# A fifth tile for loaded weight pieces, tables kept per mixer, and a later split of the attention probabilities

## The chip, the cores and the metric

The kernel runs on one core of a Trainium2 chip. The metric is the device time of one execution in microseconds (us); the time of a kernel is the median of its runs. Engines go by the profile's names: PE is the matrix engine (TensorE), PEld its loading of stationary operands, DVE is VectorE, ACT is ScalarE, POOL is GpSimd, and SP is SyncE, which here only issues transfers. "pm" is a PSUM tile of a projection.

## The reference

Two layers of a decoder trunk, 256 tokens of width 2048, all in float32:

```python
for l in range(DEPTH):
    h = rms_norm(x, mix_norm[l])
    if l % 2 == 0: h = mixer_ab(h, ...)   # causal gMLP (8 heads) beside HGRN2 (8 heads), then w_out
    else:          h = mixer_c(h, ...)    # forgetting attention, 16 heads of 128, output gate, then w_out
    x = x + h
    x = x + conv_ffn(rms_norm(x, ffn_norm[l]), ...)   # hidden 5632, causal width-3 convolution, silu(a) * b
```

The attention of one head, in blocks of 128 queries, is `p = softmax(q k^T * scale + c_t - c_s)` under a causal mask, and `o = p v`; q and k are normalised over a head's 128 values, c is the running sum of the log of a forget gate. The output is the residual stream after both layers.

## The kernel before

**Weights in three products.** All large products are made with float32 split in two: a weight piece w, 128 x 1024 and 512 KB, is loaded by a transfer of the SP queue (`weights`, L200), ACT copies it rounded into wh (L187), DVE makes the rest wl = w - wh (L188), and PE makes three products, wh with the high half of the activations, wl with the high half, wh with the low half (L362, L363, L364 in `project_four`; L343 to L345 in `project_tok`; L318 in `project`; L238 and L262 in the first projection). A piece takes 12 matmuls of 512 columns. `three` gives a piece its tiles: w from a pool with 4 slots, wh and wl from one with 3 each; inside the attention mixer each fourth piece has wh and wl in a further slot, and in the MLPs two of five pieces have all three tiles in a further pool with 2 slots each. The transfer of a piece waits until its slot is free, that is until the wl of the piece that had the slot before has been made.

**Order.** The program is written as one sequence of projections. Before each piece `tick` advances one step: it lets each of a few Python generators (for a head, a group of heads, a gate) write its next part of the small work between two pieces. When the program is built, a planner sets the order of the instructions on each engine and each queue from estimated times; edges that are added by hand hold some of it: pieces stay in order, and an operation marked `held` comes on its engine after the wh or wl of the piece last written. On the chip each queue then runs strictly in that order, waiting on semaphores.

**Turning blocks.** Activations come out of the projections with tokens on the partitions and are needed the other way. `blocks` transposes 32 x 32 blocks on DVE (L375), `moves` sends 16 transfers of 32 KB that put them in place (L382), half on SP's queue and half on POOL's. On SP they share the queue with the weights.

**The attention mixer** (`mixer_c`). Four groups of four heads; a group has three projections (q, k, v) of 8 pieces, so 24 steps. `turn_rows` scales, normalises and turns q and k. `attend` takes a pair of heads: high and low halves of q and k (L1050 to L1054), scores (L1061, L1064), forget terms and mask (L1069 to L1073), maximum, exponential with the sums of the rows into rs, 32 x 32 transposes into ptmp (L1087), 16 moves on POOL's queue into pt (L1096); then it lets `LAG + 2`, that is 8, steps pass, and splits the turned probabilities: ph on ACT (L1105), pl on DVE (L1106). One step later follow the products with v (L1114, L1117) and two copies on ACT (L1121). A second pair starts 5 steps after the first. After the groups come four projections for the output gate (w_cg), each followed by a `gate` that turns its rows and multiplies the heads' output (L1200) into yc, which is split (L414, L416); the output projection (w_co) reads yc. Gates after the first begin to multiply when all heads are done.

**Small tiles and tables.** `cst` holds the identity, a triangular mask and the causal mask of the attention for the whole kernel. In the first mixer `ss`, `Rr` and `sos` are three small tiles (factors of the gMLP's norm, reversed per-token factors, factors of HGRN2's output norm), `junk` holds squares, `tot` (2 slots) the running products of HGRN2's decay, and `ar` (3 slots) mirrored activations. In the attention mixer each of the four groups has a tile `rs` for the sums of its rows.

Of the kernel before, what the change touches and what calls it, by code (L numbers as in the profile page):

```python
# [8 lines left out]
F32 = mybir.dt.float32  # L9
# [3 lines left out]
ALU = mybir.AluOpType  # L13
AX = mybir.AxisListType

P = 128
S = 256
D = 2048
KT = D // P
NH = 8  # L20
CH = 16
# [4 lines left out]
LAG = 6  # L26
# [8 lines left out]
LANE = 64  # L35
SMALL = 4
LEVELS = (64, 32, 16, 8, 4, 2, 1)
NL = len(LEVELS)
# [8 lines left out]
K_ID, K_TRI, K_CM, K_REV = 0, 128, 256, 384  # L47
# [8 lines left out]
def tile_trunk(ctx: ExitStack, tc: tile.TileContext, x, pp_d, cst_d, mlev_d, msk_d,  # L56
               w_v, w_f, w_g, w_i, w_q, w_u, w_abo, w_cf, w_cqkv, w_cg, w_co, w_up, w_dn, spw_d, spb_d, out):
    nc = tc.nc
    V, SC, PE = nc.vector, nc.scalar, nc.tensor
# [9 lines left out]
    def nm(base):  # L69
        count[0] += 1  # L70
        return f"{base}_{count[0]}"
# [6 lines left out]
        xT += [t[:, i] for i in range(n)]  # L78
    part = {c0 + i: (t, i, c0 + n - 1) for t, c0, n in xload for i in range(n)}
    pp = cp.tile([P, -(-NPP // LANE) * LANE], F32, tag="pp", name="pp")  # L80
    cst = cp.tile([P, K_REV], F32, tag="cst", name="cst")
    ones = cp.tile([P, P], F32, tag="ones", name="ones")
    one1 = ones[:, 0:1]

    SC.dma_start(pp[:, 0:C_FFN], pp_d[:, 0:C_FFN])
    V.memset(ones, 1.0)
    ident = cst[:, K_ID:K_ID + P]

    order = mybir.DependencyInfo(mybir.DependencyClass.NoSync, mybir.DependencyReason.DATA)
    epoch = {"set": None, "load": None, "ops": []}  # L90
# [72 lines left out]

    def three(n):
        deep["turn"] += 1
        wpool, pool, nw, ns = wp, wp, 4, 3
        if deep["pool"] is not None:
            if deep["more"] == 2 and deep["turn"] > 12 and deep["turn"] % 5 in (1, 3):
                wpool, pool, nw, ns = deep["pool"], deep["pool"], 2, 2
            elif deep["more"] == 1 and deep["turn"] % 4 == 3:  # L170
                pool, ns = deep["pool"], 1
        w = wpool.tile([P, n], F32, tag="w", name=nm("w"), bufs=nw)
        wh = pool.tile([P, n], F32R, tag="wh", name=nm("wh"), bufs=ns)
        wl = pool.tile([P, n], F32R, tag="wl", name=nm("wl"), bufs=ns)
        return w, wh, wl
# [230 lines left out]
    def held(r, last="wh"):  # L406

        tc.add_manual_dep(r.ins, deep[last].ins.name, order, reason="not before")
# [98 lines left out]
    def mixer_ab(norm):  # L507
# [35 lines left out]
        def fetch_late(*args):  # L543
            r = SC.dma_start(*args)
            tc.add_manual_dep(r.ins, deep["hold"].ins.name, order, reason="queue order")

        fetch_late(cst, cst_d[:, 0:K_REV])
        fetch_late(pp[:, C_FFN:C_CW], pp_d[:, C_FFN:C_CW])
        def wide(n):
            return hp.tile([P, 1024], F32, tag="QK", name=nm(n), bufs=2)  # L550
# [9 lines left out]

        def tables():
            yield
            near, tri = kst[:, (NL - 1) * P:NL * P], cst[:, K_TRI:K_TRI + P]
            held(V.tensor_copy(msk, kst), "wl")
            nc.gpsimd.tensor_tensor(two[:, 0], near, tri, ALU.mult)
            nc.gpsimd.tensor_tensor(two[:, 1], near, two[:, 0], ALU.subtract)
            nc.gpsimd.tensor_tensor(two, two, ident.unsqueeze(1).to_broadcast([P, 2, P]), ALU.add)
            yield
            held(V.tensor_tensor(wt[0], wt[0], cst[:, K_TRI:K_TRI + P].unsqueeze(1)
                                 .to_broadcast([P, NH, P]), ALU.mult), "wl")  # L570

        mg = [keep("mg") for _ in range(NH)]

# [13 lines left out]
                                   wt[1][:, h].unsqueeze(1).to_broadcast([P, 2, P]),  # L587
                                   ALU.mult, ALU.add)

        ss = hp.tile([P, LANE], F32, tag="ss", name="ss")  # L590

        def mixes():
            while norm.Rt is None:
                yield
            for g in (1, 0):
                for T in range(2):
                    yield
                    held(act(cols2(gv[g][:, T]), of_two(last[T]) if g else cols2(gv[0][:, T]), AF.Gelu,
                             scale=norm.Rt[:, T:T + 1]))
            yield  # L600
            for g in (1, 0):
                for T in range(2):
                    i = (2 * g + T) * 4
                    j = hp.tile([P, 512], F32, tag="junk", name=nm("junk"), bufs=1)
                    held(V.tensor_tensor(j, gv[g][:, T], gv[g][:, T], ALU.mult), "wl")
                    V.tensor_reduce(ss[:, i:i + 4], j.rearrange("p (h d) -> p h d", d=P), AX.X, ALU.add)
                    yield
            yield
            rsq(ss[:, 0:2 * NH], ss[:, 0:2 * NH], P)
            for g in range(2):  # L610
                yield
                for T in range(2):
                    i = (2 * g + T) * 4
                    v4 = gv[g][:, T].rearrange("p (h d) -> p h d", d=P)
                    held(V.tensor_tensor(v4, v4, ss[:, i:i + 4].unsqueeze(2).to_broadcast([P, 4, P]),
                                         ALU.mult), "wl")
            yield
            yield
            for h in range(0, NH, 2):
                ps = bank()  # L620
                both = [mix(h + i, ps[:, i * S:(i + 1) * S]) for i in range(2)]
                for m in both:
                    next(m)
                for m in both:
                    next(m, None)
                yield


        Rr = hp.tile([P, LANE], F32, tag="Rr", name="Rr")[:, 0:2]
        rab = hp.tile([P, LANE], F32, tag="rab", name="rab")  # L630
        ra, rb = rab[:, 0:BLK], rab[:, BLK:2 * BLK]

# [67 lines left out]
        depth[0] = 5  # L700

        itoks, left, os_ = [], [NH], []
        sos = hp.tile([P, LANE], F32, tag="so", name="sos")[:, 0:2 * NH].rearrange("p (j t h) -> p j t h", j=2, t=2)


        H = P // 2
# [234 lines left out]
    def mixer_c(norm):  # L941
# [3 lines left out]
        deep.update(pool=es.enter_context(tc.tile_pool(name="cw", bufs=1)), turn=0, more=1)  # L945
        A = norm.a
        w2 = hp.tile([P, KT, CH], F32, tag="w2", name="w2")

        def fetch():
            for _ in range(FORGET):  # L950
# [86 lines left out]
        def attend(hs, q, k, v, o, rs, mark):  # L1037
# [28 lines left out]
            for i, (h, sp) in enumerate(zip(hs, sps)):  # L1066
                c0 = 3 * P * i
                parts = ((c0, c0 + P), (c0 + P, c0 + 3 * P))
                V.scalar_tensor_tensor(scf[:, c0:c0 + P], sp[:, 0:P], ct[:, 0, h:h + 1], cb[:, h % 8, 0:P],  # L1069
                                       ALU.add, ALU.subtract)  # L1070
                V.scalar_tensor_tensor(sc[:, 3 * i + 1:3 * i + 3], view(sp, P, (1, 2), (2, P)), ct[:, 1, h:h + 1],
                                       cb[:, h % 8].rearrange("p (t n) -> p t n", t=2), ALU.add, ALU.subtract)
                V.tensor_tensor(sc[:, 3 * i:3 * i + 3:2], sc[:, 3 * i:3 * i + 3:2],  # L1073
                                cst[:, K_CM:K_CM + P].unsqueeze(1).to_broadcast([P, 2, P]), ALU.add)
                mxs = hp.tile([P, LANE], F32, tag="mxs", name=nm("mxs"), bufs=2)[:, 0:2]
                sms = rs[:, :, h % 4:h % 4 + 1]
                for T, (a, b) in enumerate(parts):
                    V.tensor_reduce(mxs[:, T:T + 1], scf[:, a:b], AX.X, ALU.max, negate=True)
                for T, (a, b) in enumerate(parts):
                    act(scf[:, a:b], scf[:, a:b], AF.Exp, bias=mxs[:, T:T + 1], accum_out=sms[:, T])  # L1080
                sums.append(sms)
# [12 lines left out]
            for a in range(4):  # L1094
# [3 lines left out]
                                        .rearrange("p (m r) -> p m r", m=6))  # L1098
                if a == 1:
                    yield  # L1100
            for _ in range(LAG + 2):
                yield
            pair = [hp.tile([P, 2, S], F32R, tag=n, name=nm(n), bufs=1) for n in ("ph", "pl")]
            near = pt.rearrange("p (i m) q -> p i (m q)", i=2)[:, :, 0:S]
# [28 lines left out]
        def turn_rows(ps, ss, j, dst, mark):  # L1133
# [12 lines left out]
            transposed(lambda T: z[:, T], tmp, dst)  # L1146
            mark.append(steps[0])

        for g in range(CH // 4):
            qkv, mark = [], []  # L1150
            ss = hp.tile([P, 2, 2, LANE // 4], F32, tag="ss", name=nm("ss"), bufs=2)[..., 0:4]
            for j in range(3):
                if g == 0 and j == 2:
                    cd = []
                    queue.append(sums(*forget()))
                if g and j == 2:
                    spread(g)
                ps = early[j] if g == 0 and j < 2 else project_tok(w_cqkv[j * (CH // 4) + g], norm)
                if j == 2:
                    vs = [hp.tile([P, 512], F32R, tag=n, name=nm(n), bufs=2) for n in ("vh", "vl")]  # L1160
                    v1 = hp.tile([P, 512], F32, tag="v", name=nm("v"), bufs=2)
                    SC.activation(cols2(vs[0]), of_two(ps[0]), AF.Copy, scale=Rt[:, 0:1])
                    SC.activation(cols2(v1), of_two(ps[1]), AF.Copy, scale=Rt[:, 1:2])
                    V.scalar_tensor_tensor(cols2(vs[1]), of_two(ps[0]), Rt[:, 0:1], cols2(vs[0]).bitcast(F32),
                                           ALU.mult, ALU.subtract)
                    qkv.append((vs, v1))
                    break
                t = piece("turn", 4)
                start(turn_rows(ps, ss, j, heads(t), mark))
                qkv.append(heads(t))  # L1170
            if g == 0:
                columns(cd[1])
            os_.append(heads(piece("o", CH // 4)))
            rss.append(hp.tile([P, LANE], F32, tag="rs", name=nm("rs"), bufs=CH // 4)[:, 0:8]
                       .rearrange("p (t h) -> p t h", t=2))
            queue.extend(attend((h, h + 1), *qkv, os_[g], rss[g], mark) for h in range(4 * g, 4 * g + 4, 2))

        room, places = [], [("big", 4, 1)] + 2 * [("vh", 1, 2), ("vl", 1, 2)] + 4 * [("o", 2, CH // 4)]
# [300 lines left out]
```

## Time and profile before

| | us |
|---|---|
| median of 3 runs | 2173.42 (2173.0 to 2174.6) |
| the profiled execution's own time | 2171.18 |
| its span, first to last instruction | 2169.4 |
| PE busy in the span | 2162.7 |
| PEld, DVE, ACT, POOL busy | 1899.9, 1596.8, 1306.2, 470.1 |

The granted PE clock is full throughout. The span falls into the first mixer (to about 380), the first MLP (to about 1057), the attention mixer (to about 1510) and the second MLP. Busy PE is a modelled time: matmuls overlap, and a matmul's end is computed. So whether PE loses time is read better from the starts of two matmuls than from the idle between them. In the views, "<-" after idle time names what ended it; "SPq" is the queue of SyncE, and "x8" a run of eight merged instructions.

### The profile page before, as it was taken

The page shows a single profiled execution, that of the slowest core. Times are in us where ns is not written, and L with a number is a line of the kernel's source. Part 1 is how long each engine was busy: PE and PEld are TensorE (multiplying, and loading weights), DVE is VectorE, ACT ScalarE, POOL GpSimd, SP SyncE. Part 2 cuts the span into 40 slices and gives each one's busy share as a digit, 9 for nine tenths or more (in the row PEclk, how much of TensorE's full clock was granted, in tenths as well). Part 3 has the DMA queues.
Part 4 walks back from the last instruction along what each step waited for, and adds up shares of the span by engine and source line. Part 5 has one row for each costly group of instructions (what it writes and reads, how often), then busy time and mean ns, then how long its engine had stood idle before and what let it go on. Part 6 is the DMA issues. An engine that isn't in the chain of part 4 may idle for free.

```text
span 2169.4 us, 32511 instructions
## 1 busy us (share of the span) xinstructions
PE 2162.7 (100%) x10874; PEld 1899.9 (88%) x10874; DVE 1596.8 (74%) x2265; ACT 1306.2 (60%) x1903; POOL 470.1 (22%) x865
## 2 busy tenths in 40 slices
PE   9999999999999999999999999999999999999999
PEld 8998888888888888888888888888888888888888
DVE  7788768777577657876987787877776577667766
ACT  6677766666466545654565566666666466456642
POOL 1252231212012002111133444212211012011202
PEclk9999999999999999999999999999999999999999
DMA  8755777877667767776777767777777677766866
GB/s 299 216 174 176 213 227 236 247 231 237 212 214 228 220 215 209 236 234 200 238 229 222 225 213 223 211 242 239 236 233 229 199 236 216 229 213 209 246 214 191
DMA packets 492617, 483.55 MB, mean 223 GB/s; under 512 B 115136, under 2 KB 460368, under 8 KB 492320
## 3 DMA queue, kind: packets, MB, share of 16 engines
q1 hardware_dynamic: 465888, 453.27, 66.4%
q0 software_dynamic: 24832, 25.92, 5.2%
q10 hardware_dynamic: 1728, 2.28, 0.3%
q8 instruction: 85, 1.39, 0.3%
q14 instruction: 84, 0.69, 0.1%
HBM read 435.18 MB, written 2.11 MB: 202 GB/s over the span
## 4 chain that ended last, share of the span: by engine, by line
PE 93%; DVE 2%; DMA 2%; SPq 1%; ACT 1%; issue 1%; POOL 0%; ACTq 0%; DVEq 0%; POOLq 0%
PE pm L363 26%; PE pm L362 26%; PE pm L364 26%; PE pm L343 4%; PE pm L344 4%; PE pm L345 4%; PE pm L318 2%; PE pm L238 1%; SPq L382 1%; DVE wl L188 1%; DMA pt<-ptmp 1%; PE pm L262 0%; DMA w<-in_w_cg 0%; ACT wh L187 0%; DMA w<-in_w_co 0%
## 5 line engine op out<-in xcount | busy, mean ns | idle before, releaser
L188 DVE TENSOR_TENSOR wl<-w,wh 128x1024 fp32r<-128x1024 f32 (+1 forms) x820 | 990.4, 1217 | 451.6 <-ACT wh L187 437.9
L187 ACT ACTIVATE wh<-w 128x1024 fp32r<-128x1024 f32 (+1 forms) x820 | 855.8, 1049 | 615.4 <-PE pm L364 423.0
L363 PE MATMUL pm<-wl,a 128*128 128x512 f32 x1728 | 655.4, 379 | 0.8 <-DVE wl L188 0.8
L362 PE MATMUL pm<-wh,a 128*128 128x512 f32 x1728 | 655.8, 379 | 0.0
L364 PE MATMUL pm<-wh,a 128*128 128x512 f32 x1728 | 654.9, 379 | 0.0
L382 POOL DMA_DIRECT2D zt<-tmp x413 | 223.5, 549 | 1134.1 <-DVE tmp L375 1022.3
L363 PEld LDWEIGHTS pm<-wl,a 128*128 128x128 f32 x1728 | 326.6, 189 | 48.4 <-DVE wl L188 2.5
L362 PEld LDWEIGHTS pm<-wh,a 128*128 128x128 f32 x1728 | 326.6, 189 | 46.3
L364 PEld LDWEIGHTS pm<-wh,a 128*128 128x128 f32 x1728 | 326.6, 189 | 46.2
L362 PE MATMUL pm<-wh,hid 128*128 128x512 f32 x688 | 260.8, 379 | 0.0
L363 PE MATMUL pm<-wl,hid 128*128 128x512 f32 x688 | 260.8, 379 | 0.0
L364 PE MATMUL pm<-wh,hid 128*128 128x512 f32 x688 | 260.8, 379 | 0.0
L343 PE MATMUL pm<-wh,a 128*128 128x512 f32 x416 | 158.7, 381 | 0.0
L344 PE MATMUL pm<-wl,a 128*128 128x512 f32 x416 | 157.8, 379 | 0.1
L345 PE MATMUL pm<-wh,a 128*128 128x512 f32 x416 | 157.8, 379 | 0.0
L363 PEld LDWEIGHTS pm<-wl,hid 128*128 128x128 f32 x688 | 130.0, 189 | 18.5
L362 PEld LDWEIGHTS pm<-wh,hid 128*128 128x128 f32 x688 | 130.0, 189 | 18.4
L364 PEld LDWEIGHTS pm<-wh,hid 128*128 128x128 f32 x688 | 130.0, 189 | 18.4
L382 POOL DMA_DIRECT2D turn<-tmp x160 | 86.9, 550 | 243.3 <-DVE tmp L375 172.7
L1285 ACT ACTIVATE conv<-zt,pp 128x256 f32<-128x256 f32 x176 | 95.8, 589 | 66.3 <-DMA zt<-tmp 43.5
L1286 DVE SCALAR_TENSOR_TENSOR conv<-zt,pp,conv 128x255 f32<-128x255 f32 x176 | 80.2, 480 | 50.0 <-ACT conv L1285 40.4
L375 DVE STREAM_TRANSPOSE tmp<-z 128x512 f32<-128x512 f32 x120 | 97.8, 854 | 5.5 <-ACT z L1271 5.3
(253 smaller groups left out, 2205.7 us busy)
## 6 DMA issues: line engine op xcount, KB each, us to landing
w<-in_w_up SPq DMA_DIRECT2D x352, 512.0 KB, 4.9
w<-in_w_dn SPq DMA_DIRECT2D x176, 512.0 KB, 4.9
w<-in_w_cqkv SPq DMA_DIRECT2D x96, 512.0 KB, 4.8
w<-in_w_abo SPq DMA_DIRECT2D x32, 512.0 KB, 4.8
w<-in_w_cg SPq DMA_DIRECT2D x32, 512.0 KB, 4.7
w<-in_w_co SPq DMA_DIRECT2D x32, 512.0 KB, 4.9
zt<-tmp SPq DMA_DIRECT2D x414, 32.0 KB, 2.6
zt<-tmp POOLq DMA_DIRECT2D x413, 32.0 KB, 2.5
```

The costliest lines, as they stand in the source:

```text
L187: r = deep["wh"] = SC.activation(wh, w, AF.Copy)
L188: deep["wl"] = V.tensor_tensor(wl, w, wh.bitcast(F32), ALU.subtract)
L343: PE.matmul(to_two(ps[T]), ah, h, start=k + i == 0, stop=False)
L344: PE.matmul(to_two(ps[T]), ah, l, start=False, stop=False)
L345: deep["last"] = PE.matmul(to_two(ps[T]), al, h, start=False, stop=k + i == KT - 1)
L362: PE.matmul(to_rows(ps[T]), ah, h, start=not begun and k + i == ks[0], stop=False)
L363: PE.matmul(to_rows(ps[T]), ah, l, start=False, stop=False)
L364: deep["mm"] = deep["last"] = PE.matmul(to_rows(ps[T]), al, h, start=False, stop=not more and k + i == ks[-1] + 1)
L375: V.transpose(tmp.rearrange("p (b m i t) -> p b m i t", b=4, m=4, t=2)[:, :, :, :, T], src(T).rearrange("p (m b j) -> p b m j", m=4, b=4))
L382: queues[(a + b) % len(queues)].dma_start(dst[BLK * b:BLK * (b + 1), :, a * n:(a + 1) * n], tmp[BLK * a:BLK * (a + 1), b * 4 * n:(b + 1) * ...
L1285: held(SC.activation(c, z, AF.Identity, bias=pp[:, cb:cb + 1], scale=w(2)))
L1286: V.scalar_tensor_tensor(c[:, 1:], z[:, :S - 1], w(1), c[:, 1:], ALU.mult, ALU.add)
```

## The change

The pool of loaded pieces w has 5 slots in place of 4, for all pieces that do not use a further pool. Room for it (4 KB on each partition) comes from the small tiles: the constants are no longer kept for the whole kernel (1.5 KB), but loaded by each mixer that reads them, in the first mixer into a slot of `tot` by one transfer on ACT's queue, in the attention mixer into a tile of its own by two transfers of 64 KB on POOL's queue; the squares go into a slot of `ar` in place of `junk` (2 KB); `ss`, `Rr` and `sos` become parts of one tile, and the four `rs` parts of another. And `attend` lets `LAG + 5` steps pass, 11 in place of 8, ahead of the split of the probabilities.

```diff
 def three(n):
-        wpool, pool, nw, ns = wp, wp, 4, 3
+        wpool, pool, nw, ns = wp, wp, 5, 3
 ...
 # tile_trunk
-    cst = cp.tile([P, K_REV], F32, tag="cst", name="cst")
-    ident = cst[:, K_ID:K_ID + P]
 # mixer_ab
-        fetch_late(cst, cst_d[:, 0:K_REV])
+        cst = hp.tile([P, S], F32, tag="tot", name="cst", bufs=2)
+        ident, tri = cst[:, K_ID:K_ID + P], cst[:, K_TRI:K_TRI + P]
+        fetch_late(cst, cst_d[:, 0:S])
-        ss = hp.tile([P, LANE], F32, tag="ss", name="ss")
+        small = hp.tile([P, LANE], F32, tag="ss", name="small")
+        ss = small[:, 0:2 * NH]
-                    j = hp.tile([P, 512], F32, tag="junk", name=nm("junk"), bufs=1)
+                    j = hp.tile([P, 512], F32, tag="ar", name=nm("junk"), bufs=3)
-        Rr = hp.tile([P, LANE], F32, tag="Rr", name="Rr")[:, 0:2]
+        Rr = small[:, 4 * NH:4 * NH + 2]
-        sos = hp.tile([P, LANE], F32, tag="so", name="sos")[:, 0:2 * NH].rearrange(...)
+        sos = small[:, 2 * NH:4 * NH].rearrange(...)
 # mixer_c
+        cst = hp.tile([P, S], F32, tag="cst", name="cst")
+        ident, cm = cst[:, 0:P], cst[:, P:S]
+        nc.gpsimd.dma_start(ident, cst_d[:, K_ID:K_ID + P])
+        nc.gpsimd.dma_start(cm, cst_d[:, K_CM:K_CM + P])
 ...
 # attend
-            for _ in range(LAG + 2):
+            for _ in range(LAG + 5):
                 yield
 ...
+        rsum = hp.tile([P, LANE], F32, tag="rs", name="rsum")
-            rss.append(hp.tile([P, LANE], F32, tag="rs", name=nm("rs"), bufs=CH // 4)[:, 0:8]
-                       .rearrange("p (t h) -> p t h", t=2))
+            rss.append(rsum[:, 8 * g:8 * g + 8].rearrange("p (t h) -> p t h", t=2))
```

More of the change, by code (lines that the diff above doesn't have):

```diff
@@ L562, in tables @@
             yield
-            near, tri = kst[:, (NL - 1) * P:NL * P], cst[:, K_TRI:K_TRI + P]
+            near = kst[:, (NL - 1) * P:NL * P]
             held(V.tensor_copy(msk, kst), "wl")
@@ L568, in tables @@
             yield
-            held(V.tensor_tensor(wt[0], wt[0], cst[:, K_TRI:K_TRI + P].unsqueeze(1)
-                                 .to_broadcast([P, NH, P]), ALU.mult), "wl")
+            held(V.tensor_tensor(wt[0], wt[0], tri.unsqueeze(1).to_broadcast([P, NH, P]), ALU.mult), "wl")
         mg = [keep("mg") for _ in range(NH)]
@@ L608, in mixes @@
             yield
-            rsq(ss[:, 0:2 * NH], ss[:, 0:2 * NH], P)
+            rsq(ss, ss, P)
             for g in range(2):
@@ L702, in mixer_ab @@
         itoks, left, os_ = [], [NH], []
-        sos = hp.tile([P, LANE], F32, tag="so", name="sos")[:, 0:2 * NH].rearrange("p (j t h) -> p j t h", j=2, t=2)
+        sos = small[:, 2 * NH:4 * NH].rearrange("p (j t h) -> p j t h", j=2, t=2)
         H = P // 2
@@ L1073, in attend @@
                 V.tensor_tensor(sc[:, 3 * i:3 * i + 3:2], sc[:, 3 * i:3 * i + 3:2],
-                                cst[:, K_CM:K_CM + P].unsqueeze(1).to_broadcast([P, 2, P]), ALU.add)
+                                cm.unsqueeze(1).to_broadcast([P, 2, P]), ALU.add)
                 mxs = hp.tile([P, LANE], F32, tag="mxs", name=nm("mxs"), bufs=2)[:, 0:2]
```

## The prediction

> **What bounds the kernel now.** I read the page first, then the waits of TensorE, then TensorE in order of time around each wait, and from there backward: VectorE, then the queue of SyncE.
>
> ```profile
> span 2169.4 us, 32511 instructions
> PE 2162.7 (100%) x10874; PEld 1899.9 (88%) x10874; DVE 1596.8 (74%) x2265; ACT 1306.2 (60%) x1903; POOL 470.1 (22%) x865
> ...
> PE 93%; DVE 2%; DMA 2%; SPq 1%; ACT 1%; issue 1%; POOL 0%; ACTq 0%; DVEq 0%; POOLq 0%
> ```
>
> TensorE is busy for 2162.7 of 2169.4 us and is 93% of the chain that ended last. Whatever the edit does on other engines, it can only take away time in which TensorE stands. The waits of TensorE name what it stands for, and the merged chain gives its pace:
>
> ```profile
> PE pm L363 <- DVE wl L188: 1.4, 3, 0.7
> ```
>
> ```profile
> 15.70 31.08 PE pm L238 x144
> ```
>
> 144 matmuls of 512 columns took 31.08 us, 0.216 each; a piece of weights is 12 of them, 2.59 us, and this is also one "step" of the program. A matmul's end is modelled and overlaps the next one's start, so the 1.4 us of visible idle is less than what is lost. I take the loss from start to start instead:
>
> ```profile
> 238.81 0.38 PE L362 MATMUL pm<-wh,a 128*128 128x512 f32 x1
> ...
> 239.57 0.38 PE L364 MATMUL pm<-wh,a 128*128 128x512 f32 x1
> ...
> 1246.41 0.38 PE L343 MATMUL pm<-wh,a 128*128 128x512 f32 x1
> ...
> 1247.16 0.38 PE L345 MATMUL pm<-wh,a 128*128 128x512 f32 x1
> ...
> 1313.47 0.38 PE L362 MATMUL pm<-wh,a 128*128 128x512 f32 x1
> 1314.20 0.48 PE L363 MATMUL pm<-wl,a 128*128 128x512 f32 x1 [0.35 <-DVE wl L188]
> 1314.52 0.38 PE L364 MATMUL pm<-wh,a 128*128 128x512 f32 x1
> ...
> 1361.50 0.38 PE L362 MATMUL pm<-wh,a 128*128 128x512 f32 x1
> 1362.28 0.48 PE L363 MATMUL pm<-wl,a 128*128 128x512 f32 x1 [0.40 <-DVE wl L188]
> 1362.60 0.38 PE L364 MATMUL pm<-wh,a 128*128 128x512 f32 x1
> ...
> 1417.68 0.38 PE L362 MATMUL pm<-wh,yc 128*128 128x512 f32 x1
> 1418.73 0.48 PE L363 MATMUL pm<-wl,yc 128*128 128x512 f32 x1 [0.68 <-DVE wl L188]
> 1419.05 0.38 PE L364 MATMUL pm<-wh,yc 128*128 128x512 f32 x1
> ```
>
> Undisturbed, the third matmul of a piece starts 2 x 0.216 = 0.43 us after the first. Here it takes 0.76 in the first stage (stall Z), and in the attention mixer 0.75 (A), 1.05 (B), 1.10 (C) and 1.37 (D). The losses are 0.33, 0.32, 0.62, 0.67 and 0.94 us; A to D make **2.55 us**, with Z 2.88. In every case the matmul that is late reads wl, the low half of a weight piece. The gated MLPs lose nothing:
>
> ```profile
> 400.00:1050.00 650.00, 650.00 (x3013) 569.01 (x3012) 462.28 (x614) 375.24 (x496) 107.74 (x200) 1.00 0.72 221
> ```
>
> (Columns: stretch, its length, busy PE, PEld, DVE, ACT, POOL, granted clock, DMA share, GB/s.) Why wl is late is seen on the queue of SyncE:
>
> ```profile
> 1228.77 0.33 SPq L200 DMA_DIRECT2D w<-in_w_cqkv  x1
> 1232.08 5.11 SPq L382 DMA_DIRECT2D turn<-tmp  x8
> 1237.29 36.60 SPq L200 DMA_DIRECT2D w<-in_w_cqkv  x17
> ...
> 1298.63 5.98 SPq L382 DMA_DIRECT2D turn<-tmp  x8
> 1304.71 14.19 SPq L200 DMA_DIRECT2D w<-in_w_cg  x9
> ...
> 1401.16 3.65 SPq L200 DMA_DIRECT2D w<-in_w_co  x2
> 1405.99 5.85 SPq L382 DMA_DIRECT2D turn<-tmp  x8
> 1411.94 7.13 SPq L200 DMA_DIRECT2D w<-in_w_co  x5
> ```
>
> and on VectorE:
>
> ```profile
> 1231.90 4.57 DVE L188 TENSOR_TENSOR wl<-w,wh 128x1024 fp32r<-128x1024 f32 x4
> 1242.31 1.23 DVE L188 TENSOR_TENSOR wl<-w,wh 128x1024 fp32r<-128x1024 f32 x1 [5.85 <-ACT wh L187]
> ...
> 1346.13 1.23 DVE L188 TENSOR_TENSOR wl<-w,wh 128x1024 fp32r<-128x1024 f32 x1 [0.66 <-ACT wh L187]
> 1351.14 1.10 DVE L1200 TENSOR_TENSOR turn<-turn,o 128x256 f32<-128x256 f32 x3 [3.79 <-DMA turn<-tmp]
> ...
> 1361.01 1.22 DVE L188 TENSOR_TENSOR wl<-w,wh 128x1024 fp32r<-128x1024 f32 x1
> 1362.12 0.69 DVE L1106 TENSOR_TENSOR pl<-pt,ph 128x512 fp32r<-128x512 f32 x1
> ...
> 1417.45 1.23 DVE L188 TENSOR_TENSOR wl<-w,wh 128x1024 fp32r<-128x1024 f32 x1 [0.60 <-ACT wh L187]
> ```
>
> Between 1228.77 and 1237.29 no weight goes out: SyncE waits for VectorE's transposes and then issues eight moves, 5.11 us. VectorE meanwhile splits the four pieces it has (1231.90 to 1236.47) and then idles 5.85 us for want of a fifth. The same gap stands before B (1298.63 to 1304.71) and before D (1405.99 to 1411.94). TensorE lives on what was split before, and runs out by 0.3 to 0.9 us.
>
> **The change part by part.**
>
> *Fifth tile for w.* A weight DMA waits for its slot, freed by the wl of the piece four before. With five slots the same event frees the slot of the piece one further on, so at each row of moves one more piece is issued ahead of them. That needs the issue order on SyncE, which is fixed when the program is built, to put it there. In the present order weights already pass moves written earlier in the code: A falls in the second piece issued after the moves, so the last piece issued before them (1228.77) is used at 1246.41 - 2 x 2.59 = 1241.2, some four pieces after the transposes at 1232 of a projection that TensorE had by then finished. So I take it that the fifth passes too. Worth: one piece, 2.59 us of TensorE work, for each gap. A, B and D need 0.32, 0.62 and 0.94, so all three go: **-1.88 us**. Bounds: 0 (the fifth goes out behind the moves) and -1.88; I take the whole, being 2.59 against at most 0.94.
>
> *Stall C* is another case. VectorE is idle for 3.79 us before 1351.14, then works without a pause past 1361.01, where the late wl stands. One wl (1.23 us) done early, in that idle time, takes 1.23 us out of the queue in front, more than the 0.67 needed. Bounds 0 and -0.67; I take **-0.67**. Z at 239 stays: there the steps between are a queue of ScalarE work, and I find no gap of SyncE before it.
>
> *Split of the probabilities, LAG + 2 to LAG + 5.* Eight times (one per pair of heads) ScalarE's ph, VectorE's pl, eight matmuls (L1114, L1117) and two evacuations (L1121) come three steps, 7.8 us, later; it issues no DMA, and no queue of SP or POOL is passed.
>
> ```profile
> L1105 ACT ACTIVATE ph<-pt x8: 613/614/630, 1139.8 to 1360.1; 128x512 fp32r<-128x512 f32 x8
> ```
>
> ```profile
> 1340.96 0.61 ACT L1105 ACTIVATE ph<-pt 128x512 fp32r<-128x512 f32 x1
> ```
>
> ```profile
> ACT ph L1105 <- DMA pt<-ptmp: 8.2, 3, 4.1
> ACT conv L1285 <- DMA zt<-tmp: 43.5, 20, 5.8
> ```
>
> ScalarE waits three times for the turned probabilities, 8.2 us in all, and the next wh is queued behind each wait. At 7.8 us later the longest, 4.1 us, is gone. ScalarE is at 60%, so this alone gives TensorE nothing; its worth is in the wl and the transposes that were queued behind. The cost: 0.61 us of ScalarE and 0.69 us of VectorE land elsewhere. The last but one pair's ph and pl (ph at 1340.96) move to about 1349, inside VectorE's 3.79 us of idle, beside the early wl: 1.23 + 0.69 = 1.92 us, which fits. The last pair's move from 1360-1362 to about 1368-1370. For the first pair of each of three groups they land on the step in which k's rows are scaled and transposed, at most 0.61 + 0.69 = 1.30 us ahead of the moves; one more piece in hand (2.59 us) covers that. Bounds: 0 and 3 x 1.30 = 3.9 us lost if the cover is missing. I take 0. What is late next: pt is held 7.8 us longer, but the next pair that needs the slot comes 24 steps after. The second gate waits for the last head; its products are emitted one step later, and the output projection starts with the first gate's.
>
> *Tables and small tiles.* The load of constants shrinks by a third on ScalarE's queue; in the attention mixer two 64 KB DMAs are new on POOL.
>
> ```profile
> 1084.61 4.32 POOL L382 DMA_DIRECT2D turn<-tmp  x8 [34.11 <-ACT z L1136]
> ```
>
> Eight issues take 4.32 us, so two take about 1.1, and POOL stands idle for 34.11 us there; queued behind them are these moves alone. The masks' first reader comes long after:
>
> ```profile
> L1073 DVE TENSOR_TENSOR sc<-sc,cst x16: 414/415/421, 1117.6 to 1333.9; 128x256 f32<-128x256 f32 x16
> ```
>
> If their space came free only after 1084.61 they would hold up the moves; it belongs to the MLP before, whose last moves POOL issued by 1084.61 - 34.11 = 1050.5. Taken as 0; bounds 0 and 1.1. The tile of squares, the per-token factors and the sums of rows share tiles with work that is over or not begun: 0, the same instructions in the same number.
>
> Sum: -1.88 - 0.67 + 0 = **-2.55 us** on the profiled execution, 2171.18 to 2168.6. The three runs have a median of 2173.42, 2.24 above it, so the same difference gives 2170.9; leaving 0.2 us of it for a near miss that moves elsewhere (Z is 0.33) I forecast **2171.1 us**.
>
> **A rule weighed.** TensorE's starts stand 0.216 us apart whether its weights are barely ready (after D) or long ready (the 650 us stretch), so I take the pace as its limit. The Trainium skill (Perfetto Trace Analysis, Identifying the Most-Contended Engine) says that matmul busy time is no measure of headroom and that weight-load busy time and MFU are. The weight loads here are 88% busy, and by that rule there would be headroom of 12%, which stands among the rivals.
>
> **The rivals.**
>
> *No gain.* The fifth weight goes out behind the moves, and the stalls stay: 2173.4. For it: the issue order is fixed at build time and cannot be read off this trace. Against: the piece at 1228.77 passed older moves.
>
> *Slower by late landings.* Five outstanding weights instead of four lie ahead of moves in the same queue. One more is 512 KB, at 221 GB/s 2.4 us, by which the turned activations of the MLPs (zt) land later. ScalarE already waits 20 times for zt, at longest 5.8 us, and TensorE loses nothing by it; beyond 5.8 us the loss begins, since wh is queued behind. If four of the 20 pass that point by the whole 2.4 us, 4 x 2.4 = 9.6 us are lost, less 2.5 gained: 2180.5. Against: in the steady state a weight goes out only when one has been split, so the queue is not longer, only one piece ahead.
> The Trainium skill (DMA: Bandwidth & Descriptors, Queues, rings and completion order) says that descriptors on one engine's ring are consumed in ring order, which is what this rival needs; no row here shows it by itself.
>
> *The pace itself improves.* The weight loads leave 2169.4 - 1899.9 = 269.5 us; were one tenth of that reachable, 27 us: 2146. Against: the constant 0.216.
>
> **How the numbers follow.** A measurement of this kernel tells about 0.2%, 4.3 us, from no change: 2169.1 to 2177.8. Forecast 0.66, of which 0.03 falls below 2169.1 by the spread of runs (2173.0 to 2174.6); no gain, with or without the 1.3 us of the moved split, 0.23; slower by late landings or a like mechanism 0.09; pace 0.02. Faster 0.05, same 0.86, slower 0.09. Low end: all of 2.88 and the lowest run, 2173.0 - 2.88 = 2170.1, less half the runs' spread of 1.6, 2169.3. High end: no gain, the highest run 2174.6 and one new stall of D's size, 2175.5. Left out is about one in ten.
>
> **What would show it.** Right: on SyncE, one more weight ahead of each row of moves; wl for the fifth piece in the idle time before 1242 and 1351; TensorE's waits down to none or one in the attention mixer; no wait of ph for pt. Wrong: the same number of weights before the moves; a TensorE wait in the MLPs, with longer waits of ScalarE for zt; moves on POOL held by the two table loads; a stall at the second pair's split.

## The result, and the profile after

The changed kernel takes 2170.18 us (median of 22 runs, 2169.31 to 2172.32), the kernel before 2173.43 us in the same session (22 runs, 2171.71 to 2174.87). The ratio is 0.9985, 95% interval [0.9979, 0.9991]: 3.3 us faster, 2.0 to 4.6 by the interval. The forecast was 2171.1 us, with a range from 2169.3 to 2175.5.

The two profiled executions lie closer together: 2171.18 us before, 2170.68 us after. In the changed kernel's views the line numbers have moved: wh and wl (L187, L188) are L185 and L186, a piece's three products (L362 to L364, L343 to L345) are L360 to L362 and L341 to L343, the weight transfers (L200) L198, the moves (L382) L380, ph and pl (L1105, L1106) L1109 and L1110. Its page begins so:

```profile
span 2168.9 us, 32423 instructions
...
PE 2162.4 (100%) x10874; PEld 1900.3 (88%) x10874; DVE 1599.7 (74%) x2265; ACT 1310.1 (60%) x1903; POOL 470.7 (22%) x867
```

All waits of TensorE after (us in total, times, longest):

```profile
PE warm L143 <- DVE ones L85: 1.1, 1, 1.1
PE pm L341 <- ACT a L398: 0.4, 1, 0.4
PE pm L260 <- ACT wh L185: 0.3, 1, 0.3
PE pm L260 <- DVE a L401: 0.2, 1, 0.2
```

The first, third and fourth lie in the first 7 us, the second at the change from the first MLP to the attention mixer (1057). The row "pm <- DVE wl", 1.4 us in three waits, is gone. The table of stretches shows it for the attention mixer (columns as in the prediction: length, then busy PE, PEld, DVE, ACT, POOL, clock, DMA share, GB/s). Before, then after:

```profile
1110.00:1310.00 200.00, 199.95 (x985) 176.50 (x984) 152.11 (x245) 113.15 (x197) 80.94 (x146) 1.00 0.70 222
1310.00:1440.00 130.00, 128.57 (x613) 112.06 (x612) 102.05 (x141) 86.30 (x123) 39.60 (x72) 1.00 0.73 220
```

```profile
1110.00:1310.00 200.00, 200.00 (x986) 176.88 (x985) 158.15 (x253) 120.33 (x205) 81.06 (x147) 1.00 0.73 228
1310.00:1440.00 130.00, 130.00 (x623) 114.36 (x622) 99.61 (x136) 84.44 (x117) 39.56 (x72) 1.00 0.74 219
```

TensorE is covered for all 330 us, and in the same 130 us it starts ten more matmuls (623 against 613). Where stall C stood, the piece after the products with v runs on, on the order of time of TensorE:

```profile
1361.84 0.38 PE L360 MATMUL pm<-wh,a 128*128 128x512 f32 x1
1362.05 0.46 PE L361 MATMUL pm<-wl,a 128*128 128x512 f32 x1
1362.35 0.38 PE L362 MATMUL pm<-wh,a 128*128 128x512 f32 x1
```

0.51 us from first to third, against 1.10 before and 0.43 undisturbed. Measured as in the prediction, from start to start beyond the usual distance of that shape (summed over all matmuls that start between 1110 and 1440 us and lose more than 0.015 us), TensorE loses 3.91 us before and 1.37 after: 2.54 less. Some 1.29 of what is left (0.97 before 1310, 0.32 behind it) stands in every kernel that has none of these stalls; below, "lost in the mixer" is this sum less 1.29: 2.62 before, 0.08 after.

Over the whole trace the loss falls by 0.80 only, 13.78 to 12.98. The other 1.74 us went at places outside the mixer: the start of the kernel (+0.51), 880 in the first MLP (+0.29), the change from the gated MLP to the attention mixer (+0.54) and the last piece (+0.40). The start lost 2.33 us in the profiled execution of before and 2.57 to 3.33 in all thirteen others of this study, so that part is this execution's. The profiled execution of before lies below all 22 runs of that session (2171.18 us, where they have 2171.71 to 2174.87): outside the mixer it loses 11.2 us, less than any of the other thirteen profiles (11.7 to 14.0). So the profiles differ by 0.5 us where the medians differ by 3.3.

### The profile page after: what moved, and what is told of

Read it like the earlier page. It is cut to its first block, busy times and chain, and to the rows that moved or that the text cites. A ratio compares the mean times of both kernels' runs of the same rounds, so it can differ in the third digit from the quotient of the medians.

```text
span 2168.9 us, 32423 instructions
## 1 busy us (share of the span) xinstructions
PE 2162.4 (100%) x10874; PEld 1900.3 (88%) x10874; DVE 1599.7 (74%) x2265; ACT 1310.1 (60%) x1903; POOL 470.7 (22%) x867
## 3 DMA queue, kind: packets, MB, share of 16 engines
q8 instruction: 85, 1.39, 0.3%
## 4 chain that ended last, share of the span: by engine, by line
PE 94%; DVE 2%; DMA 2%; SPq 1%; ACT 1%; issue 0%; DVEq 0%; ACTq 0%; POOLq 0%
PE pm L360 25%; PE pm L361 25%; PE pm L362 25%; PE pm L341 4%; PE pm L343 4%; PE pm L342 4%; PE pm L316 2%; PE pm L236 1%; DVE wl L186 1%; SPq L380 1%; DMA w<-in_w_up 1%; DMA zt<-tmp 1%; PE pm L260 0%; DVE tmp L373 0%; ACT wh L185 0%
## 5 line engine op out<-in xcount | busy, mean ns | idle before, releaser
L186 DVE TENSOR_TENSOR wl<-w,wh 128x1024 fp32r<-128x1024 f32 (+1 forms) x820 | 991.6, 1217 | 460.6 <-ACT wh L185 451.1
L185 ACT ACTIVATE wh<-w 128x1024 fp32r<-128x1024 f32 (+1 forms) x820 | 856.7, 1049 | 624.4 <-PE pm L362 459.3
L360 PE MATMUL pm<-wh,a 128*128 128x512 f32 x1728 | 655.8, 379 | 0.0
L362 PE MATMUL pm<-wh,a 128*128 128x512 f32 x1728 | 654.9, 379 | 0.0
L380 POOL DMA_DIRECT2D zt<-tmp x413 | 223.5, 549 | 1134.8 <-DVE tmp L373 1022.9
L362 PEld LDWEIGHTS pm<-wh,a 128*128 128x128 f32 x1728 | 326.6, 189 | 46.3
L360 PEld LDWEIGHTS pm<-wh,a 128*128 128x128 f32 x1728 | 326.6, 189 | 46.3
L360 PE MATMUL pm<-wh,hid 128*128 128x512 f32 x688 | 260.8, 379 | 0.0
L362 PE MATMUL pm<-wh,hid 128*128 128x512 f32 x688 | 260.8, 379 | 0.0
L341 PE MATMUL pm<-wh,a 128*128 128x512 f32 x416 | 158.7, 381 | 0.4 <-ACT a L398 0.4
L343 PE MATMUL pm<-wh,a 128*128 128x512 f32 x416 | 157.8, 379 | 0.0
L360 PEld LDWEIGHTS pm<-wh,hid 128*128 128x128 f32 x688 | 130.0, 189 | 18.5
L362 PEld LDWEIGHTS pm<-wh,hid 128*128 128x128 f32 x688 | 130.0, 189 | 18.4
L361 PEld LDWEIGHTS pm<-wl,hid 128*128 128x128 f32 x688 | 130.0, 189 | 18.4
L380 POOL DMA_DIRECT2D turn<-tmp x160 | 86.9, 551 | 211.4 <-DVE tmp L373 179.3
```

Of the source, the lines that this page charges most:

```text
L185: r = deep["wh"] = SC.activation(wh, w, AF.Copy)
L186: deep["wl"] = V.tensor_tensor(wl, w, wh.bitcast(F32), ALU.subtract)
L341: PE.matmul(to_two(ps[T]), ah, h, start=k + i == 0, stop=False)
L343: deep["last"] = PE.matmul(to_two(ps[T]), al, h, start=False, stop=k + i == KT - 1)
L360: PE.matmul(to_rows(ps[T]), ah, h, start=not begun and k + i == ks[0], stop=False)
L361: PE.matmul(to_rows(ps[T]), ah, l, start=False, stop=False)
```

## The experiments

Each ratio is against the kernel before on the same chip. "Steps" are the planner's, from the transposes of the probabilities to their split: 8 with LAG + 2, 11 with LAG + 5. The table gathers what the sections tell; the wait is that of ScalarE's ph for the DMA of pt, and the last column is the loss in the mixer as defined above, from one profiled execution each. Where a single stall is given below, it is the loss of the late matmul alone; counted so, A to D are 0.22, 0.51, 0.56 and 0.84 us before.

| kernel | tiles | steps | ratio to before, 95% | wait of ph, us | lost in the mixer, us |
|---|---|---|---|---|---|
| before | 4 | 8 | 1 | 8.2 | 2.62 |
| tables and room alone | 4 | 8 | 0.9999 [0.9990, 1.0008] | 8.4 | 2.99 |
| later split alone | 4 | 11 | 0.9995 [0.9986, 1.0004] | none | 1.17 |
| tables, later split | 4 | 11 | 0.9997 [0.9988, 1.0005] | none | 1.39 |
| fifth tile with its room | 5 | 8 | 1.0019 [1.0010, 1.0028] | 16.0 | 5.20 |
| no wait | 5 | 8 | 0.9988 [0.9979, 0.9997] | none | 1.14 |
| 9 steps | 5 | 9 | 0.9985 [0.9976, 0.9994] | 10.3 | 0.79 |
| 10 steps | 5 | 10 | 0.9988 [0.9979, 0.9996] | 2.5 | 0.00 |
| 10 steps again | 5 | 10 | 0.9987 [0.9979, 0.9996] | 1.5 | 0.00 |
| after | 5 | 11 | 0.9985 [0.9979, 0.9991] | none | 0.08 |
| after again | 5 | 11 | 0.9990 [0.9981, 0.9999] | none | 0.33 |
| 14 steps | 5 | 14 | 0.9989 [0.9980, 0.9998] | none | 0.07 |
| reordered queues | 5 | 8 | 0.9988 [0.9979, 0.9997] | 10.3 | 0.06 |
| reordered, four tiles | 4 | 8 | 0.9996 [0.9987, 1.0005] | 2.8 | 1.33 |

**One part alone.** The changed kernel with one or both of its two numbers set back, and the kernel before with the later split only.

Fifth tile with its room, the changed kernel with the split at the old place:

```diff
-            for _ in range(LAG + 5):
+            for _ in range(LAG + 2):
```

> The change without the later split: fifth tile and moved tables, the probabilities split 8 steps after their moves as before. If the fifth tile carries the gain: stalls A, B and D (0.32, 0.62, 0.94 us) gone, C (0.67) gone or nearly, 2.0 to 3.3 us under the kernel before, one more weight on SyncE's queue ahead of each row of moves, and ScalarE still waiting some 8 us for the turned probabilities. If the later split carries it: under 1 us gained and A to C still in the trace.

Later split alone, the kernel before with the split moved:

```diff
-            for _ in range(LAG + 2):
+            for _ in range(LAG + 5):
```

> The kernel before with the split 11 steps after the moves and nothing else. If the fifth tile carries the gain: within 0.7 us of the kernel before, stall D unchanged at 0.94 us (it lies behind all splits), A to C changed by no more than the 0.6 us by which VectorE's transposes come earlier. If the later split carries it: 1.3 to 1.6 us gained by the loss of A, B and C.

Tables and room alone, the changed kernel with both set back:

```diff
-        wpool, pool, nw, ns = wp, wp, 5, 3
+        wpool, pool, nw, ns = wp, wp, 4, 3
...
-            for _ in range(LAG + 5):
+            for _ in range(LAG + 2):
```

> Tables per mixer and shared small tiles alone, four tiles for loaded pieces and the split 8 steps after. Both theories: no change, within 0.5 us. If the room itself costs, a wait of POOL's first moves in the attention mixer for the two table loads, up to 1.1 us.

Tables, room and later split, the changed kernel with four tiles:

```diff
-        wpool, pool, nw, ns = wp, wp, 5, 3
+        wpool, pool, nw, ns = wp, wp, 4, 3
```

> The change without the fifth tile: tables moved, split 11 steps after, four tiles. If the fifth tile carries the gain: as the kernel with the later split alone, within 0.7 us of the kernel before, weights on SyncE's queue before the moves as before. If the parts only work together with the split, 1.3 us or more gained here.

Measured: 2177.39, 2171.76, 2173.03 and 2171.74 us against 2173.05. The first of these was expected by neither theory, and the second came in the time of the theory of the later split (1.3 us), but not by the stalls that it named. The tables and small tiles are worth nothing that can be measured. The fifth tile without the later split makes the kernel **slower**: by 4.3 us against before, and 1.0019 against 0.9999 beside the same kernel with four tiles, with intervals that don't touch. TensorE and ScalarE of that kernel wait so:

```profile
PE pm L342 <- DVE wl L186: 4.3, 3, 1.7
...
ACT ph L1109 <- DMA pt<-ptmp: 16.0, 4, 5.5
```

Three stalls are new, at 1163.9 (1.42 us lost), 1232.1 (1.85) and 1300.7 (1.52), one in each of three groups of heads. At the places of A to D nothing is lost, though the new stalls, some 12 us ahead of A and B, leave TensorE late there and may hide them. The later split alone saves 1.3 us by the medians, which its interval doesn't tell from nothing; its trace has A, B and D gone, nearly all of C left (0.52 us of 0.56), and some 0.4 us of new losses at 1356 and 1358:

```profile
PE pm L363 <- DVE wl L188: 1.5, 2, 1.2
```

(One of the two, 1.2 us, is a wait at 1588 in the MLP, seen in this one execution; the kernel with tables and later split has none there. The other is C.)

What makes the fifth tile dear is read on VectorE, around the second stall. First before (four tiles), then the fifth tile alone:

```profile
1221.53 1.22 DVE L188 TENSOR_TENSOR wl<-w,wh 128x1024 fp32r<-128x1024 f32 x1
...
1226.57 0.69 DVE L1106 TENSOR_TENSOR pl<-pt,ph 128x512 fp32r<-128x512 f32 x1 [3.23 <-ACT ph L1105]
...
1227.52 1.23 DVE L188 TENSOR_TENSOR wl<-w,wh 128x1024 fp32r<-128x1024 f32 x1 [0.18 <-ACT wh L187]
...
1229.26 1.30 DVE L1144 TENSOR_TENSOR z<-z,ss 128x512 f32<-128x512 f32 x2
1230.47 1.54 DVE L375 STREAM_TRANSPOSE tmp<-z 128x512 f32<-128x512 f32 x2
1231.90 4.57 DVE L188 TENSOR_TENSOR wl<-w,wh 128x1024 fp32r<-128x1024 f32 x4
```

```profile
1223.29 1.21 DVE L186 TENSOR_TENSOR wl<-w,wh 128x1024 fp32r<-128x1024 f32 x1
...
1229.18 0.69 DVE L1110 TENSOR_TENSOR pl<-pt,ph 128x512 fp32r<-128x512 f32 x1 [4.59 <-ACT ph L1109]
...
1230.39 1.29 DVE L1148 TENSOR_TENSOR z<-z,ss 128x512 f32<-128x512 f32 x2
1231.60 1.40 DVE L373 STREAM_TRANSPOSE tmp<-z 128x512 f32<-128x512 f32 x2
1232.92 4.58 DVE L186 TENSOR_TENSOR wl<-w,wh 128x1024 fp32r<-128x1024 f32 x4
```

The wait for ph is there in both, 3.23 and 4.59 us. But before, one wl stands right behind pl; with the fifth tile it stands behind the scaling of k's rows and the transposes. Without a wl VectorE goes from 1222.75 to 1227.52 before, 4.8 us, and from 1224.50 to 1232.92 with the fifth tile, 8.4 us. TensorE's rows there:

```profile
1232.09 0.38 PE L341 MATMUL pm<-wh,a 128*128 128x512 f32 x1
1234.16 0.48 PE L342 MATMUL pm<-wl,a 128*128 128x512 f32 x1 [1.69 <-DVE wl L186]
```

On ScalarE the same: before, ph is followed by one wh and only then by the small ops of the row scaling; with the fifth tile these come directly behind ph, and four wh behind them. Before, then the fifth tile alone:

```profile
1225.91 0.63 ACT L1105 ACTIVATE ph<-pt 128x512 fp32r<-128x512 f32 x1 [4.09 <-DMA pt<-ptmp]
1226.44 1.04 ACT L187 ACTIVATE wh<-w 128x1024 fp32r<-128x1024 f32 x1
1227.39 0.19 ACT L99 ACTIVATE ss<-rm 128x8 f32<-128x8 f32 x1
```

```profile
1228.52 0.63 ACT L1109 ACTIVATE ph<-pt 128x512 fp32r<-128x512 f32 x1 [5.52 <-DMA pt<-ptmp]
...
1229.28 0.21 ACT L97 ACTIVATE ss<-ss 128x8 f32<-128x8 f32 x1
1229.39 3.95 ACT L185 ACTIVATE wh<-w 128x1024 fp32r<-128x1024 f32 x4
```

A rival is that TensorE stood for want of loaded weights: on SyncE the row of moves waits for the late transposes too, and no weight goes out from 1224.87 to 1238.28, 13.4 us. But four pieces were loaded: ScalarE makes four wh and VectorE four wl without a pause as soon as the queue lets them. The kernel with the tables and room and four tiles has the order of before, so it is the number of tiles that makes the planner put this one wl elsewhere. Why it does was not followed up.

**No wait.** The fifth tile with the split at the old place, but ph and pl are made from the blocks as they stand before the DMA that turns them.

```diff
-            near = pt.rearrange("p (i m) q -> p i (m q)", i=2)[:, :, 0:S]
+            near = tmp.rearrange("p (i m) -> p i m", i=2)[:, :, 0:S]
```

In this kernel two of the three parts of the product with v (those with ph and pl) use unturned blocks of the probabilities, so that its output is another; the amount of work is the same.

> The fifth tile and the tables with the split 8 steps after the moves, but ph and pl read the transposed blocks (ptmp) in place of the moved ones (pt), so that neither waits for the moves; the products with v then use unturned blocks in two of their three parts. Same instructions, same sizes, same steps. If the wait is the cause: ScalarE waits 0 us before ph, the three stalls are gone, 2 to 3.5 us under the kernel before. If crowding at 8 steps, or the longer queue of weights, is the cause: still 3 to 5 us slower than before.

Measured 2170.08 us, against 2172.62 for before and 2177.39 for the same kernel with the wait. The three stalls are gone:

```profile
PE pm L361 <- DVE wl L186: 1.2, 2, 0.9
```

What is left are one at 1362 (C's place, 1.04 us lost) and one at 880 (0.47). So the wait for pt, with what stands behind it, is what made the fifth tile slower, and not the tile's transfers. C comes back here behind a later VectorE: the first gate's products (L1204) wait 2.85 us for a DMA and begin at 1353.47, in the changed kernel after 1.39 us at 1351.67. Whether that alone brings C back, and why that DMA is late, is open.

**How far the split must move.** The changed kernel with 9 steps instead of 11, and in the same way with 10 (LAG + 4) and 14 (LAG + 8):

```diff
-            for _ in range(LAG + 5):
+            for _ in range(LAG + 3):
```

> The change with the split 9 steps after its moves in place of 11 (five tiles, tables moved). If the cost of the fifth tile is ScalarE's wait for the turned probabilities, with wh queued behind: one step takes 2.59 us off each wait, so the longest falls from 5.5 to about 3 us and the three stalls of 1.4 to 1.9 us go or fall below 0.3 us; time within 1 us of the kernel before or under it. If the cost is the place of the 1.3 us of splitting work: still 3 us or more slower than the change.

> The same with 10 steps. If it is the wait: longest wait under 0.5 us, no stall behind it, the time of the change within 0.5 us. If it is the place: between the kernel with 9 steps and the change.

> The same with 14 steps. If it is the wait: nothing more to gain, the time of the change within 0.5 us, unless the second gate, which waits for the last head, comes late (its products three steps later; up to 1 us). If the place of the splitting work matters: another pattern of stalls in the attention mixer, 1 us or more either way.

Measured 2169.72, 2169.62 and 2170.14 us against 2172.62: nothing between them, nor against 11 steps. The times are those of the theory of the wait; the longest waits are longer than it said (with 9 steps 4.3 us where it had 3, with 10 steps 1.1 where it had 0.5), and with 9 steps one stall of 0.42 us is left. The waits of the kernel with 9 steps:

```profile
PE pm L342 <- DVE wl L186: 0.3, 1, 0.3
...
ACT ph L1109 <- DMA pt<-ptmp: 10.3, 4, 4.3
```

and with 10:

```profile
ACT ph L1109 <- DMA pt<-ptmp: 2.5, 4, 1.1
```

One step is enough for nearly all of it. With 9 steps ph still waits, longer in sum than before (10.3 against 8.2 us), and TensorE loses 0.8 us in the mixer instead of 5.2. A wait's length therefore doesn't tell its price.

**Reordered queues.** The wait stays (8 steps), but what stood behind it goes ahead: two order edges put ph behind the last exponential of the row scaling on ScalarE, and pl behind the last transpose of its block on VectorE.

```diff
-            for _ in range(LAG + 5):
+            for _ in range(LAG + 2):
...
-            held(SC.activation(pair[0], near, AF.Copy))
-            held(V.tensor_tensor(pair[1], near, pair[0].bitcast(F32), ALU.subtract), "wl")
+            hi = SC.activation(pair[0], near, AF.Copy)
+            lo = V.tensor_tensor(pair[1], near, pair[0].bitcast(F32), ALU.subtract)
+            for r, what in ((hi, "wh"), (hi, "rsq"), (lo, "wl"), (lo, "turned")):
+                held(r, what)
```

(`deep["rsq"]` and `deep["turned"]` hold those two instructions.) The second kernel is the same with four tiles.

> Five tiles for loaded weight pieces and the split of the probabilities two steps later than the transposes' earliest (8 steps, as the fifth tile alone had it), with one edit: the planner places ph also behind the last exponential of the row scaling, and pl also behind the last transpose of its block, so that the row scaling and the transposes are no longer queued behind the two waiting instructions. Theory of the queue behind the wait: the three stalls of 1.42, 1.85 and 1.52 us at 1163.9, 1232.1 and 1300.7 fall to 0.5 us or less each, although ph still waits for pt, and the time comes to 2171 to 2173.5 us, 4 to 6 us under the fifth tile alone. Rival, the length of the wait itself decides whatever stands behind it: the stalls stay at 1 us or more and the time stays 3 to 4 us over the kernel before. If the edit also moves ph so late that its wait is gone, the run tells nothing between the two, and only repeats the longer distance.

> Four tiles for loaded weight pieces instead of five, otherwise the kernel of the reordered queues: the split of the probabilities 8 steps behind the transposes, ph behind the last exponential of the row scaling, pl behind the last transpose of its block. Beside it in the trace stands the same kernel without the two order edges (tables and room, four tiles), which loses 1.12 us beyond the pace from 1110 to 1310 and 1.87 us from 1310 to 1440. Theory, the order does it and the fifth tile adds a little: most of that goes, one stall of about 0.5 to 1 us is left near 1362, where with the longer distance and four tiles 0.5 us was left; time 2170.5 to 2172. Rival, the fifth tile is what feeds TensorE over the gap: three or four stalls stay, 2 to 3 us together, and the time is within 1 us of the kernel before, about 2172.5. Rival, the fifth tile is of no use once the order is right: no stall, and the time of the five tiles, 1 to 3.5 us under the kernel before at most 0.3 us from them.

Measured with five tiles: 2169.94 us against 2172.56, 1 us under the least that was expected; ratio 0.9988, where the fifth tile without the edges has 1.0019 with an interval that lies wholly above. ScalarE still waits, TensorE no longer does in the mixer:

```profile
PE pm L316 <- DVE wl L186: 0.2, 1, 0.2
...
ACT ph L1109 <- DMA pt<-ptmp: 10.3, 4, 3.7
```

(The wait for L316 is at the last piece of the kernel.) VectorE around the second pair:

```profile
1221.80 1.22 DVE L186 TENSOR_TENSOR wl<-w,wh 128x1024 fp32r<-128x1024 f32 x1
...
1224.22 1.29 DVE L1150 TENSOR_TENSOR z<-z,ss 128x512 f32<-128x512 f32 x2
1225.43 1.57 DVE L373 STREAM_TRANSPOSE tmp<-z 128x512 f32<-128x512 f32 x2
1228.00 0.69 DVE L1110 TENSOR_TENSOR pl<-pt,ph 128x512 fp32r<-128x512 f32 x1 [0.99 <-ACT ph L1109]
1228.94 4.63 DVE L186 TENSOR_TENSOR wl<-w,wh 128x1024 fp32r<-128x1024 f32 x4 [0.26 <-ACT wh L185]
```

The scaling and the transposes now fill the time in which pl can't start, and VectorE goes 5.9 us without a wl instead of 8.4. ph's own wait begins later, so it is shorter (3.7 us at its longest, 5.5 without the edges), but ph itself doesn't start earlier: 9.08 pieces of TensorE's work behind its transposes, 8.97 without the edges. That settles between the wait's end and its queue: the end stayed, the queue behind it went, and 5.1 of the 5.2 us lost in the mixer went with it.

With four tiles: 2171.84 us against 2173.20, and two stalls of VectorE's making are left in the mixer, C (0.70 us lost) and one at D's place (0.42); two small ones stand in the first stage.

```profile
PE pm L361 <- DVE wl L186: 1.2, 4, 0.5
```

So once the order is right, the fifth tile takes 1.27 us of loss away (1.33 to 0.06), and 1.31 with the later split (1.39 to 0.08): the same amount in two arrangements. In the times it is about a microsecond, and the intervals overlap.

**The changed kernel again, beside 10 steps.**

> The changed kernel once more, beside the 10 step distance. Theory: 2.5 to 3.5 us under the kernel before, no stall of pm for wl in the attention mixer. The stall at the change from the MLP to the attention mixer (1056.8, 0.58 us) belongs to one execution and does not come back, if it was chance; it comes back at the same place if it belongs to the program.

> Fifth tile, tables per mixer, split of the probabilities 10 steps behind the transposes instead of 11. Theory: once the wait of ph is shorter than the stock of split weights (2.5, 4 and 1.1 us here before) one step more or less changes nothing: within 0.7 us of the 11 steps. Rival: each step of earlier split frees work before the end, and it is 1 us or more faster than 11 steps.

Measured 2170.40 and 2170.21 us against 2172.56: no difference between 10 and 11 steps. The gain of the changed kernel is 2.2 us this time (0.9990 [0.9981, 0.9999]), a little under the 2.5 that were expected. The stall at the change to the attention mixer came again with 11 steps:

```profile
PE pm L341 <- ACT a L398: 0.3, 1, 0.3
```

and no such wait is listed in the two executions with 10. The kernels with 14 steps and without the wait have it too. It costs about 0.5 us, so it was not chance for this kernel, though too small to show in a time; what causes it is open.

## Why the prediction was right, and where not

The time was right: 2.55 us expected in the mixer, 2.54 found there in the trace, 2.0 to 4.6 in the times. The attribution behind it was wrong in two terms, whose errors cancelled, and that is luck. Nor does the agreement of 2.55 and 2.54 bear out the terms: the four stalls were nearly all that could be lost there, so whatever empties the mixer gives that sum.

**The bound** held. TensorE has the same 0.216 us from start to start, PEld is 88% busy in both, and the rival by which the pace improves (2146 us) is out. The rule of the Trainium skill weighed there (Perfetto Trace Analysis, Identifying the Most-Contended Engine), by which weight-load time and MFU, and not matmul time, show the headroom, is not borne out in these runs: nothing of the 12% that the loads leave was gained. But no edit was aimed at the pace, so this isn't a test of the rule.

**"Fifth tile for w", −1.88 us (A, B, D).** This step failed: it left out what the fifth tile costs. Taken alone the tile costs 4.3 us. A, B and D are gone at their places, as the step said, but in three of four groups a new and larger stall, of up to 1.85 us, stands in their stead. On top of the later split, which takes A, B and D away without it, the fifth tile is worth 1.31 us in the mixer. Its mechanism is half right. The rows of moves still stop the weights for as long as before; SyncE after:

```profile
1215.82 9.45 SPq L198 DMA_DIRECT2D w<-in_w_cqkv  x7
1228.12 5.93 SPq L380 DMA_DIRECT2D turn<-tmp  x8
1234.15 13.89 SPq L198 DMA_DIRECT2D w<-in_w_cqkv  x8
```

that is 8.9 us from 1225.27 to 1234.15, where 8.2 passed before (1229.10 to 1237.29). The fifth piece does go out ahead of them: the median from a piece's issue to its first matmul, over the 68 pieces used between 1110 and 1310, is 14.0 us before, 14.3 with the later split alone, 18.4 after, one to two pieces of 2.59 us more. And VectorE's idle 5.85 us for want of a fifth piece is gone:

```profile
1227.97 2.31 DVE L186 TENSOR_TENSOR wl<-w,wh 128x1024 fp32r<-128x1024 f32 x2
1230.20 0.68 DVE L1110 TENSOR_TENSOR pl<-pt,ph 128x512 fp32r<-128x512 f32 x1
1232.39 1.22 DVE L186 TENSOR_TENSOR wl<-w,wh 128x1024 fp32r<-128x1024 f32 x1 [1.51 <-ACT wh L185]
...
1237.57 1.23 DVE L186 TENSOR_TENSOR wl<-w,wh 128x1024 fp32r<-128x1024 f32 x1 [1.36 <-ACT wh L185]
```

(These rows have the later split in them too.) But a loaded piece helps TensorE only when it is split, and the splits stand in the queues of ScalarE and VectorE behind ph and pl. The step's bounds, "0 and -1.88", had no loss in them, although the wait of ph stood quoted three paragraphs further on.

**"Split of the probabilities", "this alone gives TensorE nothing", taken as 0.** This failed too. Alone it takes 1.45 us of loss away (2.62 to 1.17: A, B and D, less 0.4 us that is new), with five tiles 5.12 (5.20 to 0.08). Why D goes with it, some 50 us behind the last split of the probabilities, isn't shown. ScalarE's share of busy time, 60%, was the argument for nothing, and it doesn't bear on this: the engine is not short of time, it stands still in order, with the next splits behind it. The text named that queue ("its worth is in the wl and the transposes that were queued behind") and then gave it no price. The bounds, 0 to 3.9 us lost, lay on the wrong side.

**"Stall C", −0.67.** The place and the term are right, and it is the fifth tile's: in the three kernels with four tiles and the later split or the reordered queues C keeps 0.50 to 0.70 us (0.56 before, counted the same way), with five tiles it is gone, but for 0.23 us in the second profile of the changed kernel and the stall of the kernel without a wait. The cause, one wl more in VectorE's idle time ahead of 1351, is seen: 3.79 us of idle before, 1.39 after. The pl of the last pair but one, which the prediction saw beside it, comes only at 1353.81, behind that idle time.

```profile
1349.06 1.23 DVE L186 TENSOR_TENSOR wl<-w,wh 128x1024 fp32r<-128x1024 f32 x1 [1.36 <-ACT wh L185]
1351.67 1.09 DVE L1204 TENSOR_TENSOR turn<-turn,o 128x256 f32<-128x256 f32 x3 [1.39 <-DMA turn<-tmp]
```

**"Tables and small tiles", 0.** Right: 0.9999 alone. The two loads take 0.58 and 0.56 us on POOL at 1060, and its moves start 24 us later.

**The rivals.** *No gain* (2173.4): its mechanism, the fifth piece behind the moves, didn't happen. *Slower by late landings* (2180.5): ScalarE waits 24 times for zt instead of 20, 6.3 us at longest instead of 5.8, and TensorE loses at most 0.3 us in the MLPs. A slower kernel was near after all, by another mechanism than the one priced: the wait of ph with the splits behind it, 4.3 us, and the later split is what kept it away.

## What to carry to other kernels

Price a wait in an in-order queue by what is queued behind it and by the stock that the next engine can live on, not by its length or by the engine's busy share: here 10.3 us of waiting cost TensorE 0.06 us in one order, and 16.0 us cost 5.2 in another. Where two edits touch the same queue, work out each one with the other left out; a buffer more can make a kernel slower if it changes where the planner puts the work that frees it. And take losses from start to start in the stage that the change touches: it gave 2.5 us, where the times of two single executions, 0.5 us apart, did not show the gain.

## Not expected of the hardware

The start of the kernel isn't the same from run to run: over the fourteen profiles TensorE lost 2.33 to 3.33 us there, a spread of a third of the effect measured here, and two executions can't be compared by their spans without taking it out. And when turned probabilities land depends on what else their queue carries: before, with the fifth tile alone, with the queues reordered and after, those of the first pair of a group land 4.9 to 6.0 pieces of TensorE's work after their transposes began (14 to 17 us), those of the second 8.1 to 9.4 (22 to 25 us). POOL's moves of the second pair, after:

```profile
1206.18 5.10 POOL L1100 DMA_DIRECT2D pt<-ptmp  x9 [4.13 <-DVE rt L429]
...
1214.20 3.25 POOL L380 DMA_DIRECT2D turn<-tmp  x6 [1.51 <-DMA pt<-ptmp]
...
1220.71 2.23 POOL L1100 DMA_DIRECT2D pt<-ptmp  x4 [1.58 <-issue]
```

The eight moves of a projection (two of them, and three of the sixteen, are in rows left out here) stand in the middle of the sixteen, with waits of their own. That these eight make the difference is read from the order; no run took them out.
